# One encoder block on one Trainium2 core: the second four products of each seven-product pair move behind the next row block of the down projection

## The chip, the cores and the metric

The kernel runs as one program on one NeuronCore of a Trainium2 chip; the other cores stand idle. The metric is the device time of one execution in microseconds (us): 1700.74 us before the change, the median of three runs (1692.85, 1700.80 and 1700.74).

Five engines run side by side and meet only at semaphores: TensorE (PE, with its weight loads as PEld), VectorE (DVE), ScalarE (ACT), GpSimd (POOL) and SyncE (SP), which issues nearly all of the DMAs.

## The reference, cut to what matters

One layer of an encoder with 256 tokens and a model width of 2048: three attention branches, a merge, and a gated MLP. The change touches only the last product of the MLP.

```python
h2 = _rmsnorm(x, ffn_norm)
u = _causal_dwconv(h2 @ w_up, conv_w, conv_b)
g, val = jnp.split(u, 2, axis=-1)
return x + (jax.nn.silu(g) * val) @ w_down      # (256, 5504) @ (5504, 2048)
```

All inputs are float32.

## The kernel before, in words

**Precision.** Every float32 operand of a product is held as a high and a low part (`hi` is the value rounded by a copy to the type fp32r, `lo` is what remains). One product of two operands is three matmuls that add into the same PSUM bank: high by high, high by low, low by high (`add`, L905). ACT makes the high part of a weight tile (`AF.Copy`), DVE makes the low part (`tensor_sub`).

**The down projection.** The activations (`fc`) are 43 blocks of 128 rows (`k` = 0 to 42), for two groups `tt` of 128 tokens. The output is made in two halves of 1024 columns (`c0`); in each half the 43 blocks of 128 x 1024 weights come in once. An ordinary block (`prepare` L810 and `eight` L913) is 4 products: two token groups by two groups of 512 columns, 12 matmuls. The blocks are taken two at a time as pairs `p`. For the nine pairs in `SEVEN` (p = 2, 4, ..., 18), `seven` (L920) does the two blocks in 7 products in place of 8, in the manner of Strassen and Winograd: three of the products (p1 and those for the cells (0, 0) and (0, 1)) take parts of the weights as they are, and four (p5, p7, p6 and the one for the cell (1, 0)) take sums of weight parts, w1 to w4. An ordinary pair stands between two such pairs, so 21 matmuls (9 + 12) and 24 matmuls (12 + 12) alternate, 45 in a cycle; there are 18 cycles over both halves.

**Preparing the weights of a pair.** `ra` and `rb` are the two raw blocks. `ha`, `la`, `hb`, `lb` are their high and low parts, `t` (four tiles of 512 columns, t0 to t3) the sums, and `tq` the high and low parts of the sums, `th` and `tl`, two of 1024 columns each. The DVE makes t0, t1, la, lb, t2, t3, tl0, tl1 in this order; ACT makes ha, hb, th0, th1.

**Buffers.** Raw blocks lie in 4 buffers (`wraw`), high parts in 3 (`whi`) and low parts in 3 (`wlo`), for pairs and ordinary blocks alike; a buffer is taken again when the last instruction that reads it has ended. Four high parts pass through three buffers in each cycle (ha, hb and those of the two ordinary blocks). `t` exists once, `tq` twice.

**What sets the order.** Every ACT, DVE and PE instruction of this stage goes through `keep`, which holds it behind all that was written before it on its engine. So each engine does its work in the order in which the code is written, and waits in place when an operand or a buffer is not there. SP issues the DMAs of the raw blocks in the order of the blocks, each when its raw buffer is free.

Of the kernel before, what the change touches and what calls it, by code (L numbers as in the profile page):

```python
# [11 lines left out]
F32 = mybir.dt.float32  # L12
# [76 lines left out]
def hybrid_block(ctx: ExitStack, tc: tile.TileContext, x, xT, mem, memT, pos, inv, prm, gqk, bg, wts, out):  # L89
# [60 lines left out]
    def w_raw(name, j, c0, n):  # L150

        at, (name_, j_, kn, c0_, n_) = next(tiles)
        assert (name_, j_, c0_, n_) == (name, j, c0, n), (name, j, c0, n)
        raw = wraw.tile([P, 1024], F32, name="raw")
        nc.sync.dma_start(raw[:, :kn * n], wts[at, :, :kn * n])
        return raw, kn
# [645 lines left out]
    with ExitStack() as fctx:  # L802
# [7 lines left out]
        def prepare(k, c0):  # L810
            raw, _ = w_raw("down", k, c0, 1024)
            hi = whl.tile([P, 1024], F32R, name="whi")
            lo = whl.tile([P, 1024], F32R, name="wlo")
            keep(nc.scalar.activation(hi, raw, AF.Copy))  # L814
            keep(nc.vector.tensor_sub(lo, raw, hi.bitcast(F32)))  # L815
            return k, hi, lo
# [44 lines left out]
        def hl(t):  # L861
            return t[:, 0, :], t[:, 1, :]

        def residual(c0):
            e = dn.tile([P, 2, 2, 512], F32, name="e")
            for tt in range(2):
                nc.sync.dma_start(e[:, tt], x2d[tt * P:(tt + 1) * P, c0:c0 + 1024])
            return e

        def share(e, p1, p5, p6, p7):  # L870

            u = dn.tile([P, 512], F32, name="u3")
            keep(nc.scalar.activation(u, p6, AF.Copy))
            yield
            keep(nc.vector.tensor_add(e[:, 0, 0], e[:, 0, 0], p1))
            keep(nc.vector.tensor_add(u, u, p1))
            yield
            for tt in range(2):
                keep(nc.vector.tensor_add(e[:, tt, 1], e[:, tt, 1], p5))
            yield  # L880
            keep(nc.vector.tensor_add(e[:, 0, 1], e[:, 0, 1], u))
            keep(nc.vector.tensor_add(u, u, p7))
            yield
            keep(nc.vector.tensor_add(e[:, 1], e[:, 1], u.unsqueeze(1).to_broadcast([P, 2, 512])))
# [4 lines left out]
        def result(e, cc, tt, a, b):  # L889
            d = flat(e, tt, a, b)  # L890
            keep(nc.vector.tensor_add(d, d, cc[tt].rearrange("p h n -> p (h n)")[:, a:b]))

        def store(e, c0, tt, a, b, queue):
            queue.dma_start(out[tt * P:(tt + 1) * P, c0 + a:c0 + b], flat(e, tt, a, b))

        class Half:
# [21 lines left out]
                             k == NFF - 1)  # L918

            def seven(self, p):  # L920
                a, b = 2 * p, 2 * p + 1
                i, end = SEVEN.index(p), p == SEVEN[-1]
                ra, rb = (w_raw("down", k, self.c0, 1024)[0] for k in (a, b))
                ha, hb = (whl.tile([P, 1024], F32R, name="whi") for _ in range(2))
                la, lb = (whl.tile([P, 1024], F32R, name="wlo") for _ in range(2))
                t = dn.tile([P, 4, 512], F32, name="t")
                tq = th_[:, turn_[0] % 2]
                turn_[0] += 1
                b11, b12, b21, b22 = ra[:, :512], ra[:, 512:], rb[:, :512], rb[:, 512:]

                def high(dst, src):
                    keep(nc.scalar.activation(dst, src, AF.Copy))  # L932

                def sub(dst, x_, y_):
                    keep(nc.vector.tensor_sub(dst, x_, y_))

                high(ha[:, :512], b11)
                high(hb, rb)
                sub(t[:, 0], b12, b11)
                sub(t[:, 1], b12, b22)  # L940
                sub(la[:, :512], b11, ha[:, :512].bitcast(F32))
                sub(lb, rb, hb.bitcast(F32))
                sub(t[:, 2], b22, t[:, 0])
                sub(t[:, 3], b21, t[:, 2])
                for q in range(2):
                    th, tl = tq[:, 0, 2 * q:2 * q + 2], tq[:, 1, 2 * q:2 * q + 2]
                    high(th, t[:, 2 * q:2 * q + 2])
                    sub(tl, t[:, 2 * q:2 * q + 2], th.bitcast(F32))
                w11 = ha[:, :512], la[:, :512]
                w21, w22 = ((hb[:, h], lb[:, h]) for h in (slice(0, 512), slice(512, 1024)))  # L950
                w1, w3, w2, w4 = (hl(tq[:, :, q]) for q in range(4))
                s1, s2, s3 = (hl(sx[:, i, q]) for q in range(3))
                a11, s4 = (hl(fc[:, a, :, tt * P:(tt + 1) * P]) for tt in range(2))
                a12, a22 = (hl(fc[:, b, :, tt * P:(tt + 1) * P]) for tt in range(2))
                p1, p5, p6, p7 = self.p
                self.add("p1", p1, a11, w11, end)
                self.add((0, 0), self.cc[0][:, 0], a12, w21, False)
                self.add((0, 1), self.cc[0][:, 1], s4, w22, False)
                self.add("p5", p5, s1, w1, end)
                self.add("p7", p7, s3, w3, end)  # L960
                self.add("p6", p6, s2, w2, end)
                self.add((1, 0), self.cc[1][:, 0], a22, w4, False)

        e, before, shares = residual(0), None, iter(())
        for c0 in range(0, D, 1024):
            if before is not None:
                ready = [prepare(0, c0)]
                for tt, h in cells:
                    result(*before, tt, h * 512, h * 512 + 512)
            half, held = Half(c0), []  # L970
            for p in range(NFF // 2 + 1):
                if p in SEVEN:
                    half.seven(p)
                    continue
                for k in range(2 * p, min(2 * p + 2, NFF)):
                    item = ready.pop(0) if ready else prepare(k, c0)
                    assert item[0] == k
                    if k < NFF - TAIL or c0 + 1024 < D:
                        half.eight(item, cells)
                    else:  # L980
                        held.append(item)
                    if k == 2 * SEVEN[-1] + 4:
                        shares = share(e, *half.p)
                    if before is None or k > 0:
                        next(shares, None)
                    if before is not None and k in (2 * SEVEN[-1] + 4, 2 * SEVEN[-1] + 5):
                        next(shares, None)
                    if before is not None and k == 3:
                        for tt, h in cells:
                            store(before[0], 0, tt, h * 512, h * 512 + 512, nc.sync)  # L990
                    if before is not None and k == 11:
                        e = residual(c0)
            before = e, half.cc
# [61 lines left out]
```

## Time and profile before

| | |
|---|---|
| median of three runs | 1700.74 us |
| time of the profiled execution | 1692.73 us |
| span in the profile, first to last instruction | 1691.0 us |
| PE busy | 1677.3 us, 99% of the span |
| DVE busy | 1166.5 us, 69% |
| ACT busy | 890.1 us, 53% |
| the down projection's blocks | some 1462 to 1688 us of the span |

Matmuls overlap in the record: one of 512 columns is shown with 0.39 us, and the next begins 0.23 us later. So the busy time of PE hides short waits; they are read from the starts of the matmuls. The same holds for DVE and ACT on a smaller scale: the next instruction begins some 0.1 us before the end shown for the one before.

### The profile page before, as it was taken

Reading aid. Unit: us, or ns where it says so; the run is one execution under the profiler, and the core shown is the slowest. Engines: PE = TensorE matmul, PEld = TensorE weight load, DVE = VectorE, ACT = ScalarE, POOL = GpSimd, SP = SyncE. Lnnn points to the kernel's source line nnn. Section 1 sums busy time; section 2 is a strip of 40 time slices with the busy share of each in tenths; the row PEclk is TensorE's granted clock in tenths of the full one; section 3 lists DMA queues with packets and bytes.
Section 4 is the critical chain, followed back from the end, with each engine's and each line's share of the span. In section 5 each row is a group of like instructions: output and inputs, shape, how many; then the busy total and the mean of one; then the engine's idle time right before and its main releaser. Section 6 shows DMA issues by size and latency. Waiting matters only on the chain.

```text
span 1691.0 us, 22382 instructions
## 1 busy us (share of the span) xinstructions
PE 1677.3 (99%) x8364; PEld 1417.0 (84%) x8364; DVE 1166.5 (69%) x1754; ACT 890.1 (53%) x1192; POOL 6.9 (0%) x58
## 2 busy tenths in 40 slices
PE   8999999999999999999999999999999999999999
PEld 6888889888888888888888888888888888888887
DVE  5786766685645445555555577777877777888887
ACT  6654544444444467644444455555555555555453
POOL 0000000000000000000000000000000000000000
PEclk9999999999999999999999999999999999999999
DMA  8865445555565555567666755555555555666764
GB/s 314 291 202 187 150 159 168 186 179 183 187 193 193 187 175 175 184 201 214 200 201 216 230 195 188 188 190 194 188 188 190 194 190 187 203 204 205 247 199 149
DMA packets 98813, 332.78 MB, mean 197 GB/s; under 512 B 11024, under 2 KB 16016, under 8 KB 98704
## 3 DMA queue, kind: packets, MB, share of 16 engines
q1 hardware_dynamic: 98128, 330.82, 59.7%
q8 instruction: 65, 1.06, 0.2%
q10 hardware_dynamic: 576, 0.53, 0.1%
q14 instruction: 44, 0.36, 0.1%
HBM read 327.11 MB, written 4.19 MB: 196 GB/s over the span
## 4 chain that ended last, share of the span: by engine, by line
PE 98%; DVE 1%; DMA 0%; issue 0%; ACT 0%; SPq 0%
PE pj L102 81%; PE pj L910 10%; PE s L102 2%; PE s L910 2%; PE o L102 1%; PE o L910 1%; PE t L910 1%; DMA raw<-in_wts 0%; PE t L560 0%; DVE wlo L166 0%; PE t L781 0%; DVE wlo L815 0%; PE t L755 0%; PE t L331 0%; PE t L682 0%
## 5 line engine op out<-in xcount | busy, mean ns | idle before, releaser
L166 DVE TENSOR_TENSOR wlo<-raw,whi 128x1024 fp32r<-128x1024 f32 (+2 forms) x503 | 613.9, 1220 | 434.1 <-ACT whi L165 433.3
L165 ACT ACTIVATE whi<-raw 128x1024 fp32r<-128x1024 f32 (+2 forms) x503 | 531.6, 1057 | 634.6 <-PE pj L102 503.5
L102 PE MATMUL pj<-whi,xc 128*128 128x512 f32 (+2 forms) x1536 | 481.1, 387 | 0.5 <-DVE xc L198 0.5
L102 PE MATMUL pj<-x2c,whi 128*128 128x512 f32 x1376 | 477.4, 391 | 0.0
L102 PE MATMUL pj<-x2c,wlo 128*128 128x256 f32 x1376 | 385.5, 280 | 0.0
L102 PEld LDWEIGHTS pj<-whi,xc 128*128 128x128 f32 x1536 | 285.2, 188 | 55.3 <-DVE xc L198 1.0
L102 PEld LDWEIGHTS pj<-x2c,whi 128*128 128x128 f32 x1376 | 257.3, 187 | 56.3
L102 PE MATMUL pj<-wlo,xc 128*128 128x512 f32 (+2 forms) x768 | 293.3, 382 | 0.0
L102 PEld LDWEIGHTS pj<-x2c,wlo 128*128 128x128 f32 x1376 | 260.1, 189 | 0.0
L102 PEld LDWEIGHTS pj<-wlo,xc 128*128 128x128 f32 x768 | 144.6, 188 | 25.8
L910 PE MATMUL pj<-whi,fc 128*128 128x512 f32 (+1 forms) x484 | 152.8, 384 | 1.7 <-DVE u L829 1.3
L910 PEld LDWEIGHTS pj<-whi,fc 128*128 128x128 f32 x484 | 90.1, 188 | 20.9 <-DVE u L829 1.7
L910 PE MATMUL pj<-wlo,fc 128*128 128x512 f32 (+1 forms) x242 | 93.0, 384 | 0.4 <-DVE wlo L815 0.4
L102 PE MATMUL pj<-whi,mc 128*128 128x512 f32 x256 | 83.1, 402 | 6.9 <-ACT whi L165 6.9
L102 PE MATMUL pj<-xc,whi 128*128 128x512 f32 x256 | 88.9, 394 | 0.0
L102 PE MATMUL pj<-whi,mg 128*128 128x512 f32 x256 | 81.2, 393 | 0.0
L102 PE MATMUL pj<-xc,wlo 128*128 128x256 f32 x256 | 70.9, 277 | 0.0
L102 PEld LDWEIGHTS pj<-whi,mc 128*128 128x128 f32 x256 | 49.6, 194 | 17.9 <-ACT whi L165 7.6
L815 DVE TENSOR_TENSOR wlo<-raw,whi 128x1024 fp32r<-128x1024 f32 x50 | 59.3, 1220 | 4.3 <-ACT whi L814 4.1
L932 ACT ACTIVATE whi<-raw 128x512 fp32r<-128x512 f32 (+1 forms) x36 | 30.2, 839 | 58.0 <-PE pj L910 57.5
L814 ACT ACTIVATE whi<-raw 128x1024 fp32r<-128x1024 f32 x50 | 50.5, 1047 | 17.9 <-PE pj L910 15.0
L102 PEld LDWEIGHTS pj<-xc,whi 128*128 128x128 f32 x256 | 48.0, 188 | 11.1
(253 smaller groups left out, 1772.7 us busy)
## 6 DMA issues: line engine op xcount, KB each, us to landing
raw<-in_wts SPq DMA_DIRECT2D x581, 512.0 KB, 3.3
th<-in_bg SPq DMA_DIRECT2D x24, 256.0 KB, 5.7
raw<-in_wts SPq DMA_DIRECT2D x5, 492.0 KB, 3.3
nat_rows<-in_mem SPq DMA_DIRECT2D x4, 512.0 KB, 6.5
nat_rows<-in_x SPq DMA_DIRECT2D x4, 512.0 KB, 7.1
xf<-in_xT SPq DMA_DIRECT2D x4, 512.0 KB, 5.0
xrow<-in_x SPq DMA_DIRECT2D x8, 256.0 KB, 4.8
x2d<-xrow SPq DMA_DIRECT2D x8, 256.0 KB, 4.2
```

Source lines behind the costliest of these rows:

```text
L102: nc.tensor.matmul(o, l, r, start=start, stop=stop, skip_group_check=True)
L165: nc.scalar.activation(hi[:, :kn * n], raw[:, :kn * n], AF.Copy)
L166: nc.vector.tensor_sub(lo[:, :kn * n], raw[:, :kn * n], hi[:, :kn * n].bitcast(F32))
L814: keep(nc.scalar.activation(hi, raw, AF.Copy))
L815: keep(nc.vector.tensor_sub(lo, raw, hi.bitcast(F32)))
L910: keep(nc.tensor.matmul(o, l[a], r[b], start=first and i == 0, stop=stop and i == 2, skip_group_check=True))
L932: keep(nc.scalar.activation(dst, src, AF.Copy))
```

## The change

`seven` becomes a generator. Up to its `yield` it loads the two raw blocks, makes ha, hb, la and lb, and issues the three products with plain weights (9 matmuls). Behind the `yield` it makes t0 to t3, th and tl, and issues the four products with sums (12 matmuls). The loop runs the first part where the pair stood, and the second part in the next (ordinary) pair, after the 12 matmuls of its first block. The number of instructions, the buffers and the DMAs stay as they were.

```diff
                 high(ha[:, :512], b11)
                 high(hb, rb)
-                sub(t[:, 0], b12, b11)
-                sub(t[:, 1], b12, b22)
                 sub(la[:, :512], b11, ha[:, :512].bitcast(F32))
                 sub(lb, rb, hb.bitcast(F32))
-                sub(t[:, 2], b22, t[:, 0])
-                sub(t[:, 3], b21, t[:, 2])
-                for q in range(2):
-                    th, tl = tq[:, 0, 2 * q:2 * q + 2], tq[:, 1, 2 * q:2 * q + 2]
-                    high(th, t[:, 2 * q:2 * q + 2])
-                    sub(tl, t[:, 2 * q:2 * q + 2], th.bitcast(F32))
...
                 self.add("p1", p1, a11, w11, end)
                 self.add((0, 0), self.cc[0][:, 0], a12, w21, False)
                 self.add((0, 1), self.cc[0][:, 1], s4, w22, False)
+                yield
+                sub(t[:, 0], b12, b11)
+                sub(t[:, 1], b12, b22)
+                sub(t[:, 2], b22, t[:, 0])
+                sub(t[:, 3], b21, t[:, 2])
+                for q in range(2):
+                    th, tl = tq[:, 0, 2 * q:2 * q + 2], tq[:, 1, 2 * q:2 * q + 2]
+                    high(th, t[:, 2 * q:2 * q + 2])
+                    sub(tl, t[:, 2 * q:2 * q + 2], th.bitcast(F32))
...
                 self.add("p5", p5, s1, w1, end)
                 self.add("p7", p7, s3, w3, end)
                 self.add("p6", p6, s2, w2, end)
...
             for p in range(NFF // 2 + 1):
                 if p in SEVEN:
-                    half.seven(p)
+                    rest = half.seven(p)
+                    next(rest)
                     continue
                 for k in range(2 * p, min(2 * p + 2, NFF)):
                     item = ready.pop(0) if ready else prepare(k, c0)
...
                         half.eight(item, cells)
                     else:
                         held.append(item)
+                    next(rest, None)
```

## Rows read from the trace of the kernel before

**Rows 1.** The page: busy time of the engines, and the shares of the chain of work that ended last.

```profile
PE 1677.3 (99%) x8364; PEld 1417.0 (84%) x8364; DVE 1166.5 (69%) x1754; ACT 890.1 (53%) x1192; POOL 6.9 (0%) x58
...
PE 98%; DVE 1%; DMA 0%; issue 0%; ACT 0%; SPq 0%
```

**Rows 2.** The same chain in order of time, in the down projection: start us, us, engine, tile, line, instructions merged. The rows with six matmuls on pj come once in each cycle; the first and the last of an unbroken series are shown for each half, with one cycle in full.

```profile
1472.20 1.36 PE pj L910 x6
...
1524.21 1.36 PE pj L910 x6
1525.57 0.85 PE s L910 x3
1527.80 6.13 PE pj L910 x27
1534.61 1.36 PE pj L910 x6
...
1555.38 1.36 PE pj L910 x6
...
1585.20 1.36 PE pj L910 x6
...
1668.27 1.36 PE pj L910 x6
```

**Rows 3.** Who waited for whom from 1462 to 1675 us: us in total, times, longest.

```profile
ACT whi L932 <- PE pj L910: 57.5, 19, 3.3
ACT thl L932 <- DVE t L935: 30.0, 18, 1.7
DVE wlo L935 <- ACT whi L932: 23.5, 18, 1.4
...
PEld s L910 <- DVE thl L935: 5.6, 18, 0.4
```

**Rows 4.** The timeline of PE and its weight loads in one cycle: the products p5 (s) and p7 (o), the first matmul of the first ordinary block, its last (with the first of the second block), and the first matmul of the next pair (t). In brackets stands idle time before.

```profile
1525.40 1.01 PE L910 MATMUL s<-thl,sx 128*128 128x512 f32 x3
1525.68 0.30 PEld L910 LDWEIGHTS s<-thl,sx 128*128 128x128 f32 x2 [0.31 <-DVE thl L935]
1526.25 0.86 PE L910 MATMUL o<-thl,sx 128*128 128x512 f32 x3
...
1528.33 0.39 PE L910 MATMUL pj<-whi,fc 128*128 128x512 f32 x1
...
1530.83 0.62 PE L910 MATMUL pj<-whi,fc 128*128 128x512 f32 x2
...
1533.77 0.39 PE L910 MATMUL t<-whi,fc 128*128 128x512 f32 x1
```

**Rows 5.** The timeline of ACT in the same cycle: th1; the high parts of two ordinary blocks; ha; hb; th0.

```profile
1524.52 1.06 ACT L932 ACTIVATE thl<-t 128x1024 fp32r<-128x1024 f32 x1 [1.67 <-DVE t L935]
1525.49 1.99 ACT L814 ACTIVATE whi<-raw 128x1024 fp32r<-128x1024 f32 x2
1527.39 0.62 ACT L932 ACTIVATE whi<-raw 128x512 fp32r<-128x512 f32 x1
1531.25 1.06 ACT L932 ACTIVATE whi<-raw 128x1024 fp32r<-128x1024 f32 x1 [3.25 <-PE pj L910]
1532.22 1.04 ACT L932 ACTIVATE thl<-t 128x1024 fp32r<-128x1024 f32 x1
```

**Rows 6.** The timeline of DVE in the same cycle: tl0 and tl1; the low parts of two ordinary blocks; t0 and t1; la; lb; t2 and t3; tl0 and tl1 of the next pair.

```profile
1524.41 2.44 DVE L935 TENSOR_TENSOR thl<-t,thl 128x1024 fp32r<-128x1024 f32 x2
1526.76 2.36 DVE L815 TENSOR_TENSOR wlo<-raw,whi 128x1024 fp32r<-128x1024 f32 x2
1529.03 1.29 DVE L935 TENSOR_TENSOR t<-raw 128x512 f32<-128x512 f32 x2
1530.23 0.69 DVE L935 TENSOR_TENSOR wlo<-raw,whi 128x512 fp32r<-128x512 f32 x1
1532.34 1.23 DVE L935 TENSOR_TENSOR wlo<-raw,whi 128x1024 fp32r<-128x1024 f32 x1 [1.42 <-ACT whi L932]
1533.48 1.41 DVE L935 TENSOR_TENSOR t<-raw,t 128x512 f32<-128x512 f32 x2
1534.81 2.44 DVE L935 TENSOR_TENSOR thl<-t,thl 128x1024 fp32r<-128x1024 f32 x2
```

**Rows 7.** The DMAs of raw blocks: the median from issue to landing over 1462 to 1675 us, and least, median and longest from 1470 to 1560 us.

```profile
raw<-in_wts SPq DMA_DIRECT2D x79, 512.0 KB, 4.3
...
DMA to landing us min/median/max: 3.1/4.0/5.6
```

**Rows 8.** One cycle as a stretch: busy us (instructions) of each engine, then granted clock, DMA share and GB/s.

```profile
1523.37:1533.77 10.40, 10.40 (x46) 8.36 (x45) 8.95 (x11) 5.49 (x6) 0.00 (x0) 1.00 0.64 196
```

**Rows 9.** The timeline of PE behind its wait at the start of the down projection.

```profile
1461.72 0.50 PE L910 MATMUL pj<-whi,fc 128*128 128x512 f32 x1 [1.28 <-DVE u L829]
1462.06 0.40 PE L910 MATMUL pj<-wlo,fc 128*128 128x512 f32 x1
```

**Rows 10.** The end of the kernel, where block 42 is first used: PE, and the low part of block 42 on DVE.

```profile
1680.30 0.61 PE L910 MATMUL pj<-whi,fc 128*128 128x512 f32 x2
1681.31 0.50 PE L910 MATMUL pj<-wlo,fc 128*128 128x512 f32 x1 [0.40 <-DVE wlo L815]
...
1680.04 1.22 DVE L815 TENSOR_TENSOR wlo<-raw,whi 128x1024 fp32r<-128x1024 f32 x1
```

More of the change, by code (lines that the diff above doesn't have):

```diff
@@ L938, in seven @@
                 high(hb, rb)
-                sub(t[:, 0], b12, b11)
-                sub(t[:, 1], b12, b22)
                 sub(la[:, :512], b11, ha[:, :512].bitcast(F32))
                 sub(lb, rb, hb.bitcast(F32))
-                sub(t[:, 2], b22, t[:, 0])
-                sub(t[:, 3], b21, t[:, 2])
-                for q in range(2):
-                    th, tl = tq[:, 0, 2 * q:2 * q + 2], tq[:, 1, 2 * q:2 * q + 2]
-                    high(th, t[:, 2 * q:2 * q + 2])
-                    sub(tl, t[:, 2 * q:2 * q + 2], th.bitcast(F32))
                 w11 = ha[:, :512], la[:, :512]
                 w21, w22 = ((hb[:, h], lb[:, h]) for h in (slice(0, 512), slice(512, 1024)))
-                w1, w3, w2, w4 = (hl(tq[:, :, q]) for q in range(4))
                 s1, s2, s3 = (hl(sx[:, i, q]) for q in range(3))
@@ L958, in seven @@
                 self.add((0, 1), self.cc[0][:, 1], s4, w22, False)
+                yield
[7 more added lines that the diff above has]
+                    sub(tl, t[:, 2 * q:2 * q + 2], th.bitcast(F32))
+                w1, w3, w2, w4 = (hl(tq[:, :, q]) for q in range(4))
                 self.add("p5", p5, s1, w1, end)
@@ L969, in hybrid_block @@
                     result(*before, tt, h * 512, h * 512 + 512)
-            half, held = Half(c0), []
+            half, held, rest = Half(c0), [], iter(())
             for p in range(NFF // 2 + 1):
                 if p in SEVEN:
-                    half.seven(p)
+                    rest = half.seven(p)
+                    next(rest)
                     continue
```

## The prediction

> **What bounds the kernel now.** I read the page first: PE is busy for 99% of the span, and 98% of the chain that ended last is PE [rows 1]. So only what lengthens or closes a gap between matmuls counts. The chain in order of time gives the length of a cycle (one seven-product pair and one ordinary pair). The reader should see the same pattern repeat: (1555.38 - 1472.20) / 8 = 10.40 us in the first half and (1668.27 - 1585.20) / 8 = 10.38 us in the second [rows 2], 10.39 in the mean. The timeline of PE gives the pitch: the 24 matmuls of the two ordinary blocks start at 1528.33, and the next pair at 1533.77, so (1533.77 - 1528.33) / 24 = 0.2267 us each [rows 4]. Forty-five of them are 10.20 us. The cycle therefore loses only 0.19 us, which over 18 cycles is 3.4 us, 0.2% of the time. The list of waits names it: 18 times the product p5 waits for tl0 [rows 3]. The 5.6 us there are the idle time of the weight loads, part of which lies under a running matmul.
>
> Why is tl0 late? ACT makes hb only when the first ordinary block has given its buffer back (a wait of 3.25 us, [rows 5]); lb, t2, t3 and tl0 follow on DVE [rows 6]. A cycle asks DVE for 8.95 us of 10.40 and ACT for 5.49 [rows 8]. Neither is full; what binds is a buffer and the order behind it.
>
> **The change, step by step.** Nothing is added or removed, so the cost is that of a new order. PE now has: first part (9 matmuls), block k (12), second part (12), block k+1 (12). DVE has la, lb, lo(k), t0 to t3, tl0, tl1, lo(k+1). ACT has ha, hb, hi(k), th0, th1, hi(k+1).
>
> *Which buffer does hi(k) take?* Four high parts pass through three buffers. When ACT comes to hi(k), ha and hb of the new pair hold two of them, not yet read. The third is that of block k+1 of the cycle before, whose last reader is the matmul just ahead of the new pair. This was so before as well, but there 21 matmuls, 4.8 us, lay between that release and the first use of block k. Now there are 9, 2.04 us. That cover must hold an ACT copy of 1.06 us [rows 5] and a DVE subtraction of 1.22 us [rows 6], and it can't.
>
> I set the first matmul of a pair to 0 and go through one cycle. The delays are from the rows. A copy that waits for a block's buffer starts 0.19 us behind the start of the matmul that follows that block (1531.25 against 1530.83 + 0.23, [rows 4, 5]). DVE follows ACT after 0.03 us (1531.25 + 1.06 to 1532.34, [rows 5, 6]). A matmul follows the DVE operand by 0.17 us: tl0 ends at 1524.41 + 1.22 = 1525.63, and the second matmul of p5 starts two pitches before 1526.25, at 1525.80 [rows 4, 6]. Back to back, DVE instructions of 1024 columns start 1.14 us apart and those of 512 columns 0.60, 0.72 where the second needs the first, as t3 needs t2 [rows 6].
>
> 1. hi(k) runs from 0.19 to 1.25, lo(k) from 1.28 to 2.50. The second matmul of block k is the first that reads the low part; it starts at 2.67 in place of 10 x 0.2267 = 2.27. Gap: 0.40 us. Block k ends at 2.67 + 11 x 0.2267 = 5.16.
> 2. t0 stands behind lo(k) on DVE, in written order: t0 at 2.42, t1 at 3.02, t2 at 3.62, t3 at 4.34, tl0 at 4.95 to 6.17. th0 needs t0 and t1 and is made by 4.80, off the path. The second matmul of p5 starts at 6.17 + 0.17 = 6.34; without a wait it would be at 5.16 + 0.23 = 5.39. Gap: 0.95 us. Before, tl0 missed its place by 0.19; now what is late is the whole row of sums, since it begins 2.4 us after the pair and not during the ordinary blocks.
> 3. th1 starts behind t3 at 5.06 and ends at 6.12; tl1 runs from 6.16 to 7.38, and its first reader (the second matmul of p6) comes at 6.34 + 6 x 0.2267 = 7.70: no wait. The second part ends at 6.34 + 11 x 0.2267 = 8.83. lo(k+1) runs from 7.29 to 8.51 and is wanted at 9.06: no wait. Block k+1 ends at 8.83 + 2.72 = 11.55.
> 4. The next pair: la at 8.43, hb on ACT by 10.5, lb by 11.7 at the latest (next paragraph), wanted at the fifth matmul, 11.55 + 0.91 = 12.46. No wait.
>
> The new cycle is 11.55 us against 10.39: +1.16, of which +1.35 are the two new gaps and -0.19 the old one. The release, one copy, one subtraction, four sums and tl0 now stand in one row that nothing overtakes, so no later block makes it good. All 18 pairs have an ordinary pair on both sides: 18 x 1.16 = 20.9 us.
>
> *The raw blocks and SP.* ra is now read until t1 (3.71) and rb until t3 (5.03). SP issues in order, so the DMAs of the next ra, rb and k go out at about 3.75, 5.06 and 5.4. At the median of 4.3 us [rows 7] they land at 8.1, 9.4 and 9.7; hb is made from 9.4 to 10.5 and lb by 11.7, and hi(k) is not wanted before 11.74. Nothing is lost, with 0.7 us to spare. At the longest landing, 5.6 us [rows 7], rb lands at 10.66, hb ends at 11.75, lb at 13.0; the fifth matmul then starts at 13.17 in place of 12.46, and as the first part overlaps the wait of step 1, the cycle grows by some 0.3 us: 18 x 0.3 = 5.4 us more. I take nothing, since most landings are nearer to the median, and keep 5.4 for the range. Below nothing is not to be had: an earlier landing finds the buffers of step 1 still taken.
>
> *The end of the kernel.* The low part of block 42 stands on DVE behind the sums of the last pair and the additions of its products (L875 to L882). Before, it ended at 1681.26 and its matmul came 0.55 us late (1681.31 for 1680.30 + 2 x 0.23, [rows 10]). Now lo(39) to lo(41) and those additions run on from 7.29, with the pitches above: seven full-length or half-length steps bring lo(42) to 14.4, its end to 15.7. It is wanted at 11.55 + 13 x 0.2267 = 14.50, so the wait is about 1.3 us, 0.8 more than before.
>
> The sum is 20.9 + 0.8 = 21.7 us. The profiled execution took 1692.7 us, so the same execution would take 1714.4. That execution lies 8.0 us under the median of the runs, 1700.74; two of the three runs are at 1700.8 and one at 1692.85. I forecast against the median: **1722.4 us**, +1.3%.
>
> Row and rule of the Trainium skill, at the old gap. The same short wait, 18 times at the same place, goes back to ACT waiting for a buffer [rows 3, 5]. The Trainium skill's page "Perfetto Trace Analysis", section "Optimization Strategy", says that the same gap repeating on the engine that should be saturated can mean that SBUF does not hold the next tile. By that rule a new order without new buffers would leave the cycle at its 10.39 us and the time at 1700.7; it speaks against a gain, and is a rival below.
>
> **The rivals.**
>
> *The products find their sums ready.* This is the other side. If lo(k) and the sums came off the path, for instance because some buffer is free earlier than I read it, the four products would begin behind 21 matmuls in place of 9 and the old wait would go: 18 x -0.19 = -3.4 us, 1697.3 us. For it speaks that DVE is idle for 1.4 us in each cycle, waiting for hb [rows 6]. Against it: it decides at the point where lo(k) ends 0.4 us sooner and the sums 0.95 sooner than in steps 1 and 2, and in the present trace the buffer of a block is waited for in the same way, 19 times, up to 3.3 us [rows 3].
>
> *The wait moves and keeps its size.* The 0.19 us of each cycle would be lost at block k in place of p5, if the 1.4 us in which DVE now waits for hb [rows 6] took up the rest of the later start: 1700.7 us. Against it: that idle time lies behind lo(k+1), where the new order has no use for it. This is what the rule on repeating gaps gives.
>
> *Only the first gap.* If the sums stood ahead of lo(k) on DVE, or the first gap were all, the cycle would gain 0.40 - 0.19 = 0.21 us: 18 x 0.21 + 0.8 = +4.6 us, 1705.3. Against it speaks the written order, which the present DVE timeline follows exactly [rows 6].
>
> *Raw blocks late.* If three transfers issued within 1.7 us land not in 5.6 but in 7 us, hb is late by a further 1.4 us in each cycle: (0.3 + 1.4) x 18 = +31 us on top, 1753. Against it: no landing of the raw blocks in the stretch is above 5.6 us [rows 7].
>
> *The clock.* Gaps might bring TensorE to its lower level; each cycle would then grow by up to 10.2 us, 184 us in all if it stayed there. The trace shows the granted clock at 1.00 with the gap of today [rows 8], and behind a wait of 1.28 us the second matmul again takes 0.40 us and starts 0.34 after the first [rows 9]; my gaps are 0.40 and 0.95. The Trainium skill's "Perfetto Trace Analysis", section "Matmul Optimizations", asks for back-to-back matmuls because the power follows the utilization; rows 9 show no such loss for gaps of this size.
>
> **How the numbers follow.** Forecast 0.72; sums ready 0.07; wait moved 0.04; first gap only 0.06; raw blocks late 0.08; clock 0.03. The forecast's own range goes from the profiled execution's level with 20% off the gaps, 1692.7 + 17 = 1710, to the median with the longest landings, 1722.4 + 5.4 = 1728. To hold the time 8 times in 10 I take in the near side of "first gap only" and a part of the late landings: 1706 to 1735. A measurement of this kernel can tell about 0.5%, 8.5 us, from no change. Slower by more than that are the forecast, the late blocks and the clock: 0.83. Within it lie the three others, save 0.02 for faster, which the whole lost time of 3.4 us does not reach: 0.15.
>
> **What would show it.** In the profile after, the cycle should be 11.5 to 11.6 us long. PE should wait for wlo of L815 (block k) some 0.4 us and for thl some 0.95 us, 18 times each; ACT at L814 should wait for PE in each cycle, and DVE for ACT ahead of lo(k). The clock stays at 1.00. Step 1 is wrong if hi(k) starts before the pair's first matmul; step 2 if t0 runs ahead of lo(k); the DMA part if ACT waits for raw. A cycle of 10.2 us would make the whole prediction wrong.

## The result, and the profile after

The changed kernel took 1714.36 us (median of four runs, 1713.86 to 1722.95) against 1700.77 us for the kernel before, measured beside it. The ratio of the means is 1.0102 with a 95% interval of 1.0059 to 1.0146 (the medians give 1.0080): slower, as forecast, and 8 us under the forecast of 1722.4. The profiled execution took 1714.32 us, its span 1712.6 us; the forecast had worked out 1714.4 for an execution that, like the one profiled before, takes 1692.7 us without the change.

Single executions of each kernel fall into two groups some 8 to 10 us apart, and the profiles show the difference in the up projection, ahead of all that is changed here; so I compare the stretch from the first matmul of the down projection to the end of the span.

The instructions of PE by tile, in the kernel before (shortest, median and longest ns, first and last start):

```profile
L910 PE MATMUL pj<-whi,fc x484: 279/389/497, 1458.9 to 1687.3; 128*128 128x512 f32 x154, 128*128 128x256 f32 x8
```

The same in the changed kernel:

```profile
L910 PE MATMUL pj<-whi,fc x484: 274/389/496, 1457.9 to 1708.9; 128*128 128x512 f32 x154, 128*128 128x256 f32 x8
```

The stretch was 1691.0 - 1458.9 = 232.1 us and is 1712.6 - 1457.9 = 254.7 us: 22.6 us more, all of it in the down projection and the end of the kernel behind it. The page of the changed kernel answers to [rows 1]:

```profile
PE 1684.3 (98%) x8364; PEld 1415.2 (83%) x8364; DVE 1167.7 (68%) x1754; ACT 894.5 (52%) x1192; POOL 6.9 (0%) x58
...
PE 90%; DVE 7%; ACT 1%; DMA 1%; issue 1%; SPq 0%; DVEq 0%; ACTq 0%
```

DVE has the same 1754 instructions and nearly the same busy time, but 7% of the chain that ended last, where it had 1%. The chain in order of time says with what, cycle by cycle (as [rows 2]):

```profile
1525.11 3.41 PE pj L910 x15
1529.64 1.23 DVE wlo L815
1530.87 1.82 DVE t L936 x3
1533.40 1.15 DVE thl L936
1536.70 3.42 PE pj L910 x15
...
1548.30 3.41 PE pj L910 x15
```

The cycle is (1548.30 - 1525.11) / 2 = 11.59 us; it was 10.39. The view leaves out short steps of the chain, so that one row of each kind is not there in every cycle. The chain leaves PE for the low part of block k (L815), the sums (three in one row; 0.71 us between the rows, from 1532.69 to 1533.40, are the fourth) and the low part of the sums (thl), and comes back to PE. Who waited for whom, from 1462 to 1697 us (as [rows 3]):

```profile
ACT thl L933 <- DVE t L936: 49.7, 36, 2.6
ACT whi L814 <- PE pj L910: 46.5, 21, 2.9
DVE wlo L815 <- ACT whi L814: 39.8, 22, 2.6
PEld s L910 <- DVE thl L936: 19.1, 18, 1.1
ACT whi L933 <- DMA raw<-in_wts: 11.9, 18, 1.2
PE s L910 <- DVE thl L936: 11.5, 18, 0.7
PEld pj L910 <- DVE wlo L815: 10.4, 18, 0.7
```

Before, hb (L932) was what waited for PE; now it is the ordinary block (L814). Two waits of PE stand in each of the 18 cycles, one for wlo of L815 (seen at the weight loads, PEld) and one for thl. One cycle on PE (as [rows 4]): the pair's first matmul, the first three of block k, the first matmul of p5, the next two, the first of p7, and the next pair.

```profile
1539.95 0.39 PE L910 MATMUL t<-whi,fc 128*128 128x512 f32 x1
...
1541.77 0.61 PE L910 MATMUL pj<-whi,fc 128*128 128x512 f32 x2
1542.53 0.50 PE L910 MATMUL pj<-wlo,fc 128*128 128x512 f32 x1
1542.86 0.63 PE L910 MATMUL pj<-whi,fc 128*128 128x512 f32 x2
...
1545.17 0.39 PE L910 MATMUL s<-thl,sx 128*128 128x512 f32 x1
1546.20 0.74 PE L910 MATMUL s<-thl,sx 128*128 128x512 f32 x2 [0.63 <-DVE thl L936]
1546.77 0.85 PE L910 MATMUL o<-thl,sx 128*128 128x512 f32 x3
...
1551.54 0.39 PE L910 MATMUL t<-whi,fc 128*128 128x512 f32 x1
```

The first row of block k holds the last matmul of the first part and the first of block k, at 1541.77 and 1542.00. The third of block k starts at 1542.86; at the pitch of 0.2267 us it would start at 1542.45. So the first gap costs 0.41 us. p7 starts at 1546.77 in place of 1545.17 + 3 x 0.2267 = 1545.85: the second gap costs 0.92 us. The first interval behind a wait is itself longer (1542.53 to 1542.86, 0.33 us in place of 0.23); both figures hold it.

ACT in that cycle (as [rows 5]): hi(k), th0, th1, and hb of the next pair.

```profile
1540.15 1.06 ACT L814 ACTIVATE whi<-raw 128x1024 fp32r<-128x1024 f32 x1 [2.89 <-PE pj L910]
1543.71 1.06 ACT L933 ACTIVATE thl<-t 128x1024 fp32r<-128x1024 f32 x1 [2.49 <-DVE t L936]
1545.04 1.06 ACT L933 ACTIVATE thl<-t 128x1024 fp32r<-128x1024 f32 x1 [0.27 <-DVE t L936]
...
1548.59 1.06 ACT L933 ACTIVATE whi<-raw 128x1024 fp32r<-128x1024 f32 x1 [1.02 <-DMA raw<-in_wts]
```

DVE (as [rows 6]): lo(k), t0 and t1, t2 and t3, tl0 and tl1, and lb of the next pair.

```profile
1541.25 1.23 DVE L815 TENSOR_TENSOR wlo<-raw,whi 128x1024 fp32r<-128x1024 f32 x1 [2.62 <-ACT whi L814]
1542.39 1.28 DVE L936 TENSOR_TENSOR t<-raw 128x512 f32<-128x512 f32 x2
1543.59 1.41 DVE L936 TENSOR_TENSOR t<-raw,t 128x512 f32<-128x512 f32 x2
1544.92 2.43 DVE L936 TENSOR_TENSOR thl<-t,thl 128x1024 fp32r<-128x1024 f32 x2
...
1549.68 1.22 DVE L936 TENSOR_TENSOR wlo<-raw,whi 128x1024 fp32r<-128x1024 f32 x1 [0.59 <-ACT whi L933]
```

From the pair's first matmul (1539.95) hi(k) starts after 0.20 us (forecast 0.19), lo(k) after 1.30 (1.28), t0 after 2.44 (2.42), tl0 after 4.97 (4.95). ACT stood idle for 2.89 us before hi(k): it waited not for data but for a buffer that PE was still reading.

### The profile page after: what moved, and what is told of

Read it like the earlier page. It is cut to its first block, busy times and chain, and to the rows that moved or that the text cites. A ratio compares the mean times of both kernels' runs of the same rounds, so it can differ in the third digit from the quotient of the medians.

```text
span 1712.6 us, 22398 instructions
## 1 busy us (share of the span) xinstructions
PE 1684.3 (98%) x8364; PEld 1415.2 (83%) x8364; DVE 1167.7 (68%) x1754; ACT 894.5 (52%) x1192; POOL 6.9 (0%) x58
## 4 chain that ended last, share of the span: by engine, by line
PE 90%; DVE 7%; ACT 1%; DMA 1%; issue 1%; SPq 0%; DVEq 0%; ACTq 0%
PE pj L102 80%; PE pj L910 5%; DVE t L936 3%; DVE wlo L815 2%; PE s L102 2%; PE s L910 1%; DVE thl L936 1%; ACT whi L814 1%; PE o L102 1%; DMA raw<-in_wts 1%; PE o L910 1%; PE t L560 0%; DVE wlo L166 0%; PE t L781 0%; PE t L755 0%
## 5 line engine op out<-in xcount | busy, mean ns | idle before, releaser
L815 DVE TENSOR_TENSOR wlo<-raw,whi 128x1024 fp32r<-128x1024 f32 x50 | 61.0, 1222 | 40.0 <-ACT whi L814 39.8
L814 ACT ACTIVATE whi<-raw 128x1024 fp32r<-128x1024 f32 x50 | 52.5, 1054 | 54.9 <-PE pj L910 48.4
L933 ACT ACTIVATE thl<-t 128x1024 fp32r<-128x1024 f32 x36 | 38.2, 1060 | 49.7 <-DVE t L936 49.7
L910 PEld LDWEIGHTS pj<-wlo,fc 128*128 128x128 f32 x242 | 45.4, 188 | 20.2 <-DVE wlo L815 11.9
```

The costliest lines, as they stand in the source:

```text
L910: keep(nc.tensor.matmul(o, l[a], r[b], start=first and i == 0, stop=stop and i == 2, skip_group_check=True))
```

## The experiments

Two causes are in the forecast: the third weight buffer, which makes hi(k) wait for the block just ahead of the pair, and the order on DVE, which puts four sums behind lo(k). Three kernels, made from the changed one, take them apart; two more, made from the kernel before, treat the old gap. Of each there is one profile, and the cycle and the stretch are read from it.

| kernel | first matmul of the down projection, us | span, us | stretch between, us | cycle, us |
|---|---|---|---|---|
| before | 1458.9 | 1691.0 | 232.1 | 10.39 |
| changed | 1457.9 | 1712.6 | 254.7 | 11.59 |
| e1: changed, ha and la apart | 1457.8 | 1688.4 | 230.6 | 10.20 |
| e2: products alone moved | 1457.3 | 1702.3 | 245.0 | 10.69 to 10.73 |
| e5: sums stay | 1466.6 | 1703.9 | 237.3 | 10.66 |
| e3: old order, t2 and t3 first | 1466.8 | 1696.1 | 229.3 | 10.20 |
| e4: old order, ha and la apart | 1464.4 | 1693.1 | 228.7 | 10.20 |

**e1: the changed order, another buffer.**

```diff
-                ha, hb = (whl.tile([P, 1024], F32R, name="whi") for _ in range(2))
-                la, lb = (whl.tile([P, 1024], F32R, name="wlo") for _ in range(2))
+                ha = dn.tile([P, 512], F32R, name="wha")
+                la = dn.tile([P, 512], F32R, name="wla")
+                hb = whl.tile([P, 1024], F32R, name="whi")
+                lb = whl.tile([P, 1024], F32R, name="wlo")
```

> The changed kernel, but with ha and la of a pair in buffers of their own (512 columns each), so that each of hb and the two ordinary blocks takes its own buffer again. Theory (the third buffer and the order behind it set the cycle): the high part of block k is made while the pair before still runs, PE no longer waits for wlo of block k nor for tl0, and the cycle falls from 11.59 us to 10.2 to 10.5 us; what is left is the loop over the raw buffers (rb free after t3, landing 4.0 to 4.3 us, hb, lb, lo(k), four sums: about 10.2 us). Against a span of 1691.0 before: 1688 to 1697. Rival (the sums behind block k on DVE cost 0.95 us by their order alone, whatever the buffers): the second gap stays, the cycle is about 11.15 us, the span about 1705.

Measured: the ratio to the kernel before is 0.9994 (0.9969 to 1.0019), the stretch 230.6 us, 24.1 less than the changed kernel's. In the repeating cycle the chain is PE alone, in steps of 10.20 us:

```profile
1542.56 4.08 PE pj L910 x18
...
1552.76 4.08 PE pj L910 x18
```

ACT makes the high part of block k early:

```profile
1546.73 1.06 ACT L814 ACTIVATE whi<-raw 128x1024 fp32r<-128x1024 f32 x1 [0.63 <-PE pj L910]
```

The pair to which that block belongs has its first matmul at 1551.92, so hi(k) starts 5.2 us ahead of it and not 0.2 behind. The sums still stand behind lo(k) on DVE, and in the repeating cycle it costs nothing. So the buffer is the root, and the order carries its delay on to tl0. (e1 gives la a buffer of its own as well, so by itself it does not part the buffers of the high parts from those of the low parts; that the high one was short is read from the changed kernel, where ACT waits 2.89 us for PE before hi(k), and lo(k) follows hi(k) after 0.04 us.) The loop over the raw buffers did not lengthen the cycle either, with one exception, the first cycle of the second half. There a raw block lands late (a step of 6.77 us on the chain at 1575.39), hi(k) with it, and both gaps are back:

```profile
1584.64 0.50 PE L910 MATMUL pj<-wlo,fc 128*128 128x512 f32 x1 [0.66 <-DVE wlo L815]
...
1588.31 0.73 PE L910 MATMUL s<-thl,sx 128*128 128x512 f32 x2 [0.65 <-DVE thl L938]
```

They cost 0.92 us each, about the 1.9 us by which the stretch of e1 is longer than that of e4 below. So in the new order a late hi(k) brings both gaps, whatever makes it late.

**e2: only the products move.** The sums, th and tl stand again ahead of the `yield`, in the old order, so that lo(k) comes behind tl1 on DVE; only the four products stay behind block k.

```diff
                 high(hb, rb)
+                sub(t[:, 0], b12, b11)
+                sub(t[:, 1], b12, b22)
                 sub(la[:, :512], b11, ha[:, :512].bitcast(F32))
                 sub(lb, rb, hb.bitcast(F32))
+                sub(t[:, 2], b22, t[:, 0])
+                sub(t[:, 3], b21, t[:, 2])
+                for q in range(2):
...
                 yield
-                sub(t[:, 0], b12, b11)
...
                 self.add("p5", p5, s1, w1, end)
```

> Only the four products move on PE; sums, th and tl stay where they were before, ahead of block k on DVE and ACT. Theory: the second gap (0.95 us) goes, since the sums are ready long before; the first one stays, because block k still waits for the buffer of the block just before the pair: lo(k) is ready 2.67 us behind the pair's first matmul in place of 2.27. Cycle 10.6 us, span 1691.0 + 18 x 0.21 + up to 0.8 = 1695 to 1696. Rival (PE's own order, 9 + 12 + 12 + 12, costs the whole 1.2 us a cycle through raw blocks or PSUM): cycle 11.5, span about 1712.

Measured: ratio 1.0069 (1.0042 to 1.0096), stretch 245.0 us. The second gap is gone and the first is left, as expected; the cycle is 10.69 to 10.73 us. But the stretch is 12.9 us longer than before where 4 to 5 were expected: a miss, and the cycle explains only 18 x 0.32 = 5.8 of it. The rest lies in the first cycle of each half. PE there, in the second half:

```profile
1591.19 0.39 PE L910 MATMUL pj<-whi,fc 128*128 128x512 f32 x1
1592.60 0.50 PE L910 MATMUL pj<-whi,fc 128*128 128x512 f32 x1 [1.02 <-ACT whi L814]
1594.05 0.76 PE L910 MATMUL pj<-wlo,fc 128*128 128x512 f32 x1 [0.95 <-DVE wlo L815]
1594.61 1.05 PE L910 MATMUL pj<-whi,fc 128*128 128x512 f32 x2
```

Two waits cost 1.18 and 1.22 us, and behind them matmuls come only every 0.42 us for some 3 us, which costs about 1.7 us more. That is 4.1 us where a later cycle loses about 0.5, and the first half loses as much: 3.64 and 3.63 us more, 7.3 together. With the 5.8 it makes 13.1, about what was measured. The reason for the waits: what comes ahead of the first pair is ordinary blocks alone, so the buffer of hb is given back one product group (12 matmuls, 2.7 us) later in relation to the pair than in a later cycle, and lb, t2, t3, tl0, tl1 and then lo(k) follow it on DVE. I had worked out only the repeating cycle.

**e5: only the sums stay.** t0 to t3 stand where they were before; th, tl and the products behind block k.

```diff
                 high(hb, rb)
+                sub(t[:, 0], b12, b11)
+                sub(t[:, 1], b12, b22)
                 sub(la[:, :512], b11, ha[:, :512].bitcast(F32))
                 sub(lb, rb, hb.bitcast(F32))
+                sub(t[:, 2], b22, t[:, 0])
+                sub(t[:, 3], b21, t[:, 2])
...
                 yield
-                sub(t[:, 0], b12, b11)
-                sub(t[:, 1], b12, b22)
-                sub(t[:, 2], b22, t[:, 0])
-                sub(t[:, 3], b21, t[:, 2])
```

> The changed kernel, but with the four sums t0 to t3 where they were before (around la and lb, ahead of block k on DVE); th, tl and the four products stay behind block k. Theory: the second gap is the time that the four sums take between lo(k) and tl0; with them gone from there tl0 ends about 3.6 us behind the pair's first matmul, 1.7 us before it is wanted, and only the first gap is left. Cycle 10.6 to 10.7 us, and no extra wait in the first cycle of a half, which e2 had, since lo(k) again stands ahead of tl0 and tl1. From the first matmul of the down projection to the end 232.1 us before, 254.7 after the change: here 237 to 239. Rival (block k, or any DVE work, between the pair's two parts keeps tl0 late): the second gap stays at 0.9 us, cycle 11.5, and the stretch is 253 or more.

Measured: ratio 1.0033 (1.0005 to 1.0062), stretch 237.3 us. The chain steps by (1634.27 - 1612.95) / 2 = 10.66 us:

```profile
1612.95 3.41 PE pj L910 x15
...
1634.27 3.41 PE pj L910 x15
```

So 0.93 us of the 1.20 that the change added to a cycle are the four sums behind lo(k), and the 0.27 that remain are the first gap less the old wait. The first cycles of the halves take 10.68 and 10.93 us, 0.5 and 0.7 more than their matmuls and not 4.1, which bears out the reading of e2.

**e3 and e4: the old order and its own gap.** e3 only puts lb behind t2 and t3 in the kernel before; e4 gives ha and la their own buffers there, with the edit of e1.

```diff
                 sub(la[:, :512], b11, ha[:, :512].bitcast(F32))
-                sub(lb, rb, hb.bitcast(F32))
                 sub(t[:, 2], b22, t[:, 0])
                 sub(t[:, 3], b21, t[:, 2])
+                sub(lb, rb, hb.bitcast(F32))
```

> The kernel before, with t2 and t3 ahead of lb on DVE: they don't need hb, so they fill the 1.42 us in which DVE waits for it. Theory: tl0 is ready 1.3 us sooner, the old wait of p5 goes, the cycle falls from 10.39 to 10.20 us: span 1691.0 - 3.4 = 1687.6. Rival (the gap only moves, since the buffer is what is short): lb is late for the cell (0, 0), the cycle stays at 10.39, the span at 1691.

> The kernel before, with ha and la in buffers of their own. Theory: hb no longer waits for block k, and the old wait of p5 goes by way of the buffers: cycle 10.20 us, span about 1687.6, the same as with the sums first. Rival (the old gap is DVE's order or its share of 86%, not the buffer): cycle 10.39, span 1691.

Measured: the ratio of e3 is 0.9983 (0.9960 to 1.0005), that of e4 0.9983 (0.9959 to 1.0006); both intervals just reach 1. Sorted, the times say more: half of the twelve of each kernel, 1687.5 to 1689.1 us, lie below the least of the 32 of the kernel before, 1690.4. The size of the gain is read from the profiles. The chain of e3:

```profile
1541.33 1.36 PE pj L910 x6
...
1551.53 1.36 PE pj L910 x6
```

and that of e4:

```profile
1538.96 1.36 PE pj L910 x6
...
1549.16 1.36 PE pj L910 x6
```

Both step by 10.20 us, 45 pitches, and PE no longer waits within a cycle; only once, near the start of the second half of e3, a wait of 0.42 us is left. Their stretches, 229.3 and 228.7 us, are 2.8 and 3.4 us shorter than before, 0.2% of the whole time; that of e1, 230.6, is 1.5 us shorter. The spans expected, 1687.6, were missed by what lies ahead of the stretch: in these two executions the down projection began 7.9 and 5.5 us later than in the kernel before. The DVE timeline of e3 shows how the idle time for hb is filled, with t2 and t3 ahead of lb:

```profile
1546.55 1.41 DVE L935 TENSOR_TENSOR t<-raw,t 128x512 f32<-128x512 f32 x2
1549.26 1.23 DVE L935 TENSOR_TENSOR wlo<-raw,whi 128x1024 fp32r<-128x1024 f32 x1 [1.30 <-ACT whi L932]
1550.41 2.35 DVE L935 TENSOR_TENSOR thl<-t,thl 128x1024 fp32r<-128x1024 f32 x2
```

Here the buffer wait still stands (1.30 us), and does no harm.

## Why the prediction was right, step by step

**The bound and the old gap: right.** The forecast gave the cycle 10.20 us of matmuls and 0.19 of waiting. e3 and e4 took the wait away in two ways and reached 10.20. So the whole prize was 3.4 us, and the changed order could not win more.

**The first gap: right.** Forecast 0.40 us, measured 0.41. In e1, where hi(k) starts 5.4 us sooner against the pair's first matmul, the gap is gone from the cycle. One delay of the working is made up otherwise than I wrote: the 0.17 us from the end of a DVE operand to the matmul are some 0.05 us (lo(k) ends at 1542.48, the matmul starts at 1542.53) and a first interval that is 0.11 us longer. The sum comes out the same.

**The second gap: right.** Forecast 0.95, measured 0.92; e5 shows that it is the four sums behind lo(k), e1 that they cost it only because lo(k) is late.

**The cycle: right, a little short.** 11.55 forecast, 11.59 measured. Most of the difference is in block k: from its third matmul (1542.86) to p5 (1545.17) ten matmuls take 0.231 us each and not 0.2267, 0.04 us in all.

**The end of the kernel: right.** Forecast a wait of 1.3 us where there were 0.55; the low part of block 42 is now wanted at 1701.21 + 2 x 0.23 = 1701.66 and its matmul starts at 1702.92, 1.26 later (as [rows 10]):

```profile
1701.21 0.61 PE L910 MATMUL pj<-whi,fc 128*128 128x512 f32 x2
1702.92 0.50 PE L910 MATMUL pj<-wlo,fc 128*128 128x512 f32 x1 [1.09 <-DVE wlo L815]
```

Together: 18 x 1.20 + 0.7 = 22.3 us of the 22.6 that the stretch grew; forecast were 21.7. That the profiled time, 1714.32, met the forecast of 1714.4 to 0.1 us is in part luck: the added cost was 0.9 us larger, and the down projection began 1.0 us sooner than in the kernel before.

**The raw blocks: right in the cost, wrong in the sign.** I had written that the DMA part is wrong if ACT waits for raw blocks. It does wait, 18 times, 11.9 us in all, because hb is now reached earlier than its block lands. Step 4 of the forecast contained that wait (hb made from the landing on), and it costs nothing: in the cycle shown lb ends at 1549.68 + 1.22 = 1550.90 and is first read by the fifth matmul of the next pair, due at 1551.54 + 0.91 = 1552.45. A better sign would have been PE waiting for wlo of lb. Only in the first cycle of the second half does a late block reach PE: the chain has one DMA there, of 6.39 us, and the first gap is 0.17 us longer. The forecast took 5.6 us for the longest landing of the stretch, but [rows 7] end at 1560 us; over 1462 to 1675 us the longest of the kernel before is 6.2 us, and it lies between 1560 and 1600 us, where the second half begins.

**The starting number: this made the 8 us.** I added 21.7 us to the median of the runs before, 1700.74, and not to the profiled 1692.73. Three of the four times of the changed kernel are at 1714.2 in the mean, 21.3 us above the one of 1692.85 before; the fourth, 1722.95, is 21.9 us above the 1701.0 of the other three before. So the added cost was right from either start; which of these times the two medians would fall on was chance.

**The rivals.** Sums found ready, the wait merely moved, and only the first gap fell with the two waits of PE per cycle; late raw blocks fell with the length of the cycle. The gap alone exists, as e5: it would have been some 5 us. The clock stayed at 1.00 over the span of the changed kernel, as its gaps of 0.41 and 0.92 us suggested; that it can matter here, e2 shows below.

**The rule on repeating gaps.** The Trainium skill's "Perfetto Trace Analysis", section "Optimization Strategy", reads a repeating gap as a possible lack of room for the next tile. The trace agrees as to the cause in e1 and e4, where 4 KB more for each partition close the gaps. It does not follow that only room helps: e3 closes the old gap with the same buffers.

## What to carry to other kernels

When a piece of work is moved away from what it stood beside, ask what it had been covering: here 12 matmuls between the release of a buffer and its next use. Count, for each buffer in the ring, which instruction gives it back and how many matmuls lie between that and the first use of its next contents; where the copies and subtractions in between take longer, their excess comes back in every cycle, with everything queued behind them in program order. Before moving products to hide a wait, look for other work of the late engine that needs no wait, as t2 and t3 did: moving one line won most of the 3.4 us that were to be had. And work out the first cycle too, not only the repeating one.

## What the runs showed of the hardware

The granted clock fell in e2 at the first pair of each half, and nowhere in the changed kernel's cycles. The stretch around the first, with busy us (instructions) of each engine, clock, DMA share and GB/s:

```profile
1471.00:1478.00 7.00, 4.97 (x15) 3.39 (x14) 6.37 (x7) 3.44 (x4) 0.00 (x0) 0.76 0.58 188
```

Within it stand two waits, 1.23 and 1.22 us lost with one matmul between them; then matmuls of 512 columns come every 0.42 to 0.43 us, and after some 3 us every 0.23 again. In the second half, from 1594.30 to 1597.00 us, where the matmuls are at that slow pitch throughout, the granted clock is 0.50: the lower of the two levels, 1.2 GHz. In the changed kernel the nearest thing, 1.26 us lost once at the end, and the 1.28 us of [rows 9] brought no such fall. So in e2 the two waits were dearer than their sum: about 1.7 us more for each half, 3.4 us in all. That it is their closeness is a reading; no run varied it. The Trainium skill's "Perfetto Trace Analysis", section "Matmul Optimizations", says that the power follows the utilization; that the granted clock fell behind these two waits agrees with it. The forecast's rival of the clock was thus no idle one, though the change did not meet it.

The up projection, which no edit touches, ran at two pitches: its 1376 matmuls of one kind were shown with a median of 391 ns in the kernel before, the changed kernel, e1 and e2, and of 398 in e3, e4 and e5. From the first of them to the last it took 1458.5 - 980.3 = 478.2 us in the kernel before and 1466.4 - 979.2 = 487.2 in e3, at the same granted clock of 1.00. In the profile of the kernel before:

```profile
L102 PE MATMUL pj<-x2c,whi x1376: 389/391/477, 980.3 to 1458.5; 128*128 128x512 f32 x197
```

and of e3:

```profile
L102 PE MATMUL pj<-x2c,whi x1376: 389/398/476, 979.2 to 1466.4; 128*128 128x512 f32 x197
```

Why one execution has the longer pitch stays open; it was not tried.
